# One kernel, three orders: forms of the gate stage, tile products of the output projection, and the forms that open the feed-forward stage

## The chip, the cores and the metric

The kernel runs on one core of a Trainium2 chip. The metric is the device time of one execution in microseconds (us). The time before is the median of three runs, 1219.32 us (1218.68 to 1220.99).

## What is computed

One block of a streaming encoder, in float32, for 1024 tokens and 16 meta tokens ahead of them, 1024 channels wide. Cut to what matters here:

```python
def hybrid_mixer(u, ...):
    z = jnp.einsum('bld,dn->bln', u, w_in)
    a, q, k, v, r, lr, ga, gb = jnp.split(z, IN_SPLITS, axis=-1)
    y_a = ...            # multi-scale pooling of a, mixed, times w_pool_out
    y_b = ...            # chunked gated linear attention of q, k, v, lr; norm; silu(r); times w_gla_out
    m = jax.nn.sigmoid(ga) * y_a + jax.nn.sigmoid(gb) * y_b
    return jnp.einsum('bld,de->ble', m, w_out)

def squared_relu_mlp(u, w_ff1, w_ff2):
    hdn = jnp.square(jax.nn.relu(jnp.einsum('bld,df->blf', u, w_ff1)))
    return jnp.einsum('blf,fd->bld', hdn, w_ff2)

h = h + hybrid_mixer(rmsnorm(h, norm_mix), ...)
h = h + squared_relu_mlp(rmsnorm(h, norm_ffn), w_ff1, w_ff2)
return rmsnorm(h, norm_final)[:, N_META:]
```

`w_ff1` is 1024 x 4096 and `w_ff2` 4096 x 1024. The change touches three stages: the first product with `w_in` (its gate columns), the product of `m` with `w_out`, and the first products with `w_ff1`.

## The kernel before

**Split products.** Every float32 operand is split into a high part that TensorE takes and a low part, the rest. ScalarE (ACT) makes the high part by a copy, VectorE (DVE) the low part by a subtraction: for weights these are `split` (L267 high, L268 low) and, for `w_out`, L1572 and L1573. A product is three matmuls for each of four blocks of the contraction, high by high, high by low and low by high (`mm3`, L249 to L251). A product of a 128-row tile with 512 columns is thus twelve matmuls.

**Seven products for eight.** The large products are done on quarters of the matrices with seven products in place of eight, P1 to P7, from sums and differences of quarters. `Quarters` does this for `w_in`'s gate columns and for `w_ff1`, column block by column block: P3.1 is the third product of block 1. `Quarters.order` lists the products; `sums` makes the sum or difference of weights that each needs on DVE, `forms` splits it, and loads the next weights once a form has freed their place (`load`, on SyncE's queue, SP, L300). The results are joined on DVE: P6 gives `u2p` (L400), P7 gives `u3p` (L405), and P3, P4 and P5 are added to these (`c`, L868, in the gate stage; `acc`, L1915, in the feed-forward stage). A form can only be written once the products of the form four places before it have been read.

**The output projection.** It runs between the attention and the feed-forward stage, token tile by token tile (0 to 3 are one half of the tokens, 4 to 7 the other). `PLAN` is a list of steps in the order in which they are given to all engines; ACT and DVE run in that order, and SP's loads do as well. In it `P1.0` is the first product of tile 0. P1 and P2 share a bank (`b[t]`), so do P5 and P3, and P7 and P4. `T1` to `T4` are sums of quarters of `w_out`, made earlier in memory (`wt_dram`); `ldT4.0` loads a half of one (L1563), always into the same two places (`rawx`, `u2p`), `T4.0a` makes its high part on ACT and `T4.0` its low part on DVE. `S1` to `S4` are sums of the tokens' quarters (L1674), `fS` their split parts (L1657 and L1664). `u` (L1768, ACT) takes a partial sum out of its bank; `C11` (L1678), `l5`, `l3`, `l7` (L1698), `a4` and `U2` (L1694) join products into `acc`; `x` and `ldx` bring in the rows of `x`, `x.4` to `x.7` by an adding DMA on GpSimd's queue (POOL). `s3` splits a tile of `s3` (L1707 low, L1709 high). `sq`, `ln` and `nm` are the norm of a tile (its last step is L241, on DVE), `t0` to `t7` its transposes on TensorE (L1807), the `e` steps the transposed parts and forms (L1809 ACT, L1810 DVE), `x4` the form of P4 (`t4h`, `t4l`, L1752). `F.0` and on are steps of the feed-forward loop: one product each, in `Quarters.order`'s order, so F.8 is P3.0, F.9 P6.1, and F.10 P4.0. `sm`, `pr` and `prl` make its weight forms: sum, high part, low part.

**Queues.** SP issues loads in the program's order. Ahead of the output projection it issued rows 0 and 3 of `x` (`behind_third`, L1855), `gB`, the gain of the norm (`load_gB`, L1551), and then T2; in the queue T4 stood behind the first two loads of `w_ff1` (`first_blocks`).

## Time and profile before

| | |
|---|---|
| median of three runs | 1219.32 us |
| the profiled execution | 1217.28 us |
| its span, first to last instruction | 1215.3 us |
| granted TensorE clock, mean | 0.997 |
| ACT busy | 648.7 us (53%) |
| POOL busy | 75.9 us (6%) |

The profiled execution is 2.0 us longer than its span and 2.0 us shorter than the median. The span is made of stages: the product with `w_in` with the gate columns first, the pooling and the attention, the output projection from about 490 to 590 us, and the feed-forward stage from about 588 us to the end. Times of the trace are counted from the span's start. A row of the timeline has the start, the length, the engine, the line and the operation, and in brackets how long the engine had stood idle and what ended that. An engine that is busy all the time sets the pace; an idle time counts only where that engine is the one.

### The profile page before, as it was taken

What the parts mean: (1) busy time and instruction counts of PE and PEld (TensorE: products, weight loads), DVE (VectorE), ACT (ScalarE), POOL (GpSimd) and SP (SyncE); (2) the same over time, 40 slices, a digit from 0 to 9 for tenths busy, and PEclk for the clock granted to TensorE, in tenths of its full rate; (3) what the DMA queues carried; (4) which work ended last, traced back from release to release, by engine and by line L of the source; (5) the groups of instructions that cost most, each with busy time, mean ns of one, the idle gap of its engine ahead of it and who ended that gap; (6) DMA issues with size and microseconds to landing.
All of it is one profiled execution on the core that took longest, in us unless ns stands there. A gap on an engine that the chain in (4) does not pass through costs nothing.

```text
span 1215.3 us, 18460 instructions
## 1 busy us (share of the span) xinstructions
PE 1183.5 (97%) x6762; PEld 986.2 (81%) x6762; DVE 896.9 (74%) x1436; ACT 648.7 (53%) x1176; POOL 75.9 (6%) x122
## 2 busy tenths in 40 slices
PE   9989999999999999989989999999999999999997
PEld 8878888898988877768768888888888888888886
DVE  7987577666677877777887667676675887887686
ACT  7677567745446433438745455454454444444554
POOL 2200010000102244010000000000000000000000
PEclk9999999999999999999999999999999999999999
DMA  8246783545108577972235444454479963333532
GB/s 256 36 113 171 218 193 120 156 122 164 37 19 279 195 246 231 355 185 112 97 121 171 145 162 156 130 166 145 166 259 322 329 232 96 96 96 95 173 96 87
DMA packets 149514, 199.02 MB, mean 164 GB/s; under 512 B 10712, under 2 KB 81136, under 8 KB 148624
## 3 DMA queue, kind: packets, MB, share of 16 engines
q1 hardware_dynamic: 144144, 181.79, 46.1%
q0 software_dynamic: 5120, 15.80, 5.7%
q8 instruction: 53, 0.87, 0.3%
q14 instruction: 37, 0.30, 0.1%
q10 hardware_dynamic: 160, 0.27, 0.1%
HBM read 138.04 MB, written 68.16 MB: 170 GB/s over the span
## 4 chain that ended last, share of the span: by engine, by line
PE 84%; DVE 6%; DMA 5%; ACT 2%; issue 1%; SPq 0%; POOL 0%; DVEq 0%; ACTq 0%; POOLq 0%
PE b_ms L250 9%; PE b_ms L251 9%; PE b_ms L249 9%; PE b_mm L249 9%; PE b_mm L251 9%; PE b_mm L250 9%; PE b_x L250 7%; PE b_x L249 7%; PE b_x L251 7%; DMA rawx<-wt_dram 2%; DMA o<-ma_dram 1%; PE b_sc L1326 1%; DMA plain_dram<-t 1%; PE b_mx L249 1%; PE b_mx L251 1%
## 5 line engine op out<-in xcount | busy, mean ns | idle before, releaser
L249 PE MATMUL b_mm<-th,w1h 128*128 128x512 f32 (+1 forms) x308 | 115.5, 375 | 5.0 <-DVE c L868 3.1
L251 PE MATMUL b_mm<-th,w1l 128*128 128x512 f32 (+1 forms) x308 | 114.2, 371 | 0.0
L250 PE MATMUL b_mm<-tl,w1h 128*128 128x512 f32 (+1 forms) x308 | 114.1, 371 | 0.0
L249 PE MATMUL b_x<-th,w1h 128*128 128x512 f32 (+1 forms) x264 | 100.2, 380 | 0.0
L250 PE MATMUL b_x<-tl,w1h 128*128 128x512 f32 (+1 forms) x264 | 100.1, 379 | 0.0
L251 PE MATMUL b_x<-th,w1l 128*128 128x512 f32 (+1 forms) x264 | 99.7, 378 | 0.0
L267 ACT ACTIVATE w1h<-raw 128x512 fp32r<-128x512 f32 x98 | 60.8, 620 | 26.8 <-PE b_ms L250 14.3
L267 ACT ACTIVATE w1h<-fs 128x512 fp32r<-128x512 f32 x78 | 49.0, 628 | 46.5 <-PE b_ms L250 27.1
L268 DVE TENSOR_TENSOR w1l<-raw,w1h 128x512 fp32r<-128x512 f32 x98 | 67.1, 685 | 8.3 <-ACT w1h L267 8.3
L249 PEld LDWEIGHTS b_mm<-th,w1h 128*128 128x128 f32 x308 | 57.8, 188 | 16.3 <-issue 6.2
L251 PEld LDWEIGHTS b_mm<-th,w1l 128*128 128x128 f32 x308 | 57.9, 188 | 10.1
L250 PEld LDWEIGHTS b_mm<-tl,w1h 128*128 128x128 f32 x308 | 57.9, 188 | 9.6
L267 ACT ACTIVATE w1h<-bt 128x512 fp32r<-128x512 f32 x44 | 27.8, 632 | 66.8 <-issue 62.5
L268 DVE TENSOR_TENSOR w1l<-fs,w1h 128x512 fp32r<-128x512 f32 x78 | 53.5, 685 | 13.4 <-ACT w1h L267 13.4
L251 PEld LDWEIGHTS b_x<-th,w1l 128*128 128x128 f32 x264 | 49.6, 188 | 9.5
L249 PEld LDWEIGHTS b_x<-th,w1h 128*128 128x128 f32 x264 | 49.6, 188 | 9.5
L250 PEld LDWEIGHTS b_x<-tl,w1h 128*128 128x128 f32 x264 | 49.6, 188 | 9.3
L1978 DVE TENSOR_TENSOR bt<-w,w 128x512 f32<-128x512 f32 x80 | 54.7, 684 | 0.3 <-DMA w<-in_w_ff_dram 0.3
L267 ACT ACTIVATE fxh<-bt 128x512 fp32r<-128x512 f32 x36 | 22.8, 632 | 56.0 <-issue 50.4
L1917 ACT ACTIVATE acc<-acc 128x512 f32<-128x512 f32 x48 | 30.3, 631 | 34.0 <-DVE acc L1915 34.0
L268 DVE TENSOR_TENSOR w1l<-rawx,w1h 128x512 fp32r<-128x512 f32 x44 | 30.1, 687 | 24.4 <-ACT w1h L267 24.4
L267 ACT ACTIVATE w1h<-rawx 128x512 fp32r<-128x512 f32 x44 | 27.5, 626 | 35.0 <-PE b_ms L250 19.9
(535 smaller groups left out, 3424.1 us busy)
## 6 DMA issues: line engine op xcount, KB each, us to landing
hf_dram<-acc SPq DMA_DIRECT2D x112, 256.0 KB, 2.1
raw<-hf_dram SPq DMA_DIRECT2D x112, 256.0 KB, 2.6
w<-in_w_ff_dram SPq DMA_DIRECT2D x64, 256.0 KB, 4.5
raw<-in_w_in_dram SPq DMA_DIRECT2D x22, 512.0 KB, 4.5
raw<-in_w_ff_dram SPq DMA_DIRECT2D x16, 512.0 KB, 4.1
rawx<-in_w_ff_dram SPq DMA_DIRECT2D x16, 512.0 KB, 4.2
wt_dram<-in_w_out_dram POOLq DMA_DIRECT2D x6, 1024.0 KB, 11.0
rawx<-in_w_in_dram SPq DMA_DIRECT2D x10, 512.0 KB, 4.4
```

The costliest lines, as they stand in the source:

```text
L249: pe.matmul(ps, ah, bh, start=first and i == 0, stop=False, skip_group_check=more)
L250: pe.matmul(ps, ah, bl, start=False, stop=False, skip_group_check=more)
L251: pe.matmul(ps, al, bh, start=False, stop=last and i == n - 1, skip_group_check=more)
L267: act.activation(hi, a, ACT.Copy)
L268: low = lambda: dve.tensor_tensor(lo, a, f32(hi), ALU.subtract)
L1326: pe.matmul(b[to, e, j], kk[r, s], qq[r, s], start=True, stop=True, tile_position=(e * CH, u * CH))
L1917: act.activation(h[w], b, ACT.Relu)
L1978: dve.tensor_tensor(bt, w, S["w2"][q[3:]][:, i], ALU.add if q[2] == "+" else ALU.subtract)
```

## The change

Three orders are changed, and some loads with them; no product is added or left out.

- **Gate stage.** `Quarters.order` gives the first products as P6.0, P7.0, P4.0, P3.0, P6.1, P1.2, where it was P6.0, P7.0, P3.0, P6.1, P4.0, P1.2. The load of the next weights' second half then waits for P3.0's form and no longer for P4.0's.
- **Feed-forward stage.** With the new flag `moved`, which is set for this stage alone, the order is P6.0, P7.0, P3.0, P6.1, P7.1, P4.0, P1.2: P7.1 now stands ahead of P4.0, where it followed P1.2. `PLAN` therefore holds one step more, F.11, which is P4.0.
- **Output projection.** `PLAN` is listed anew. The products run P1, P2, P6, P5.0, P5.1, P7.0, P3.0, P3.1, P5.2, P4.0, t0, P7.1, t1, P3.2, t4, P5.3, P4.1, t2, P7.2, P3.3, P7.3, t5, P4.2, t3, P4.3, F.0; before, P5 and P3 of all four tiles stood ahead of P7 and P4. `u.1` and `u.2` stand ahead of T2's parts; `C11.2`, `C11.3` and `C11.0` stand together, behind P2's products, and `C11.1` alone behind T4's first part.
- **Loads.** T2 goes ahead of rows 0 and 3 of `x`; `gB` goes between rows 2 and 1; T4 goes ahead of the first two loads of `w_ff1`.

```diff
@@ Quarters.order @@
-            yield from (("P6", 0), ("P7", 0), ("P3", 0), ("P6", 1), ("P4", 0))
+            moved = (("P6", 0), ("P7", 0), ("P3", 0), ("P6", 1), ("P7", 1), ("P4", 0))
+            yield from moved if self.moved else ((p, 0) for p in ("P6", "P7", "P4", "P3"))
             for i in range(2, self.n + 1):
-                for p in ("P6", "P1", "P7", "P5", "P4", "P2", "P3")[i == 2 :]:
+                for p in ("P6", "P1", "P7", "P5", "P4", "P2", "P3"):
+                    if self.moved and (p, i - 1) in moved:
+                        continue
...
@@ Quarters.forms @@
-                if p == ("P3" if i else "P4") and i + 2 < self.n:
+                if p == ("P4" if self.moved and not i else "P3") and i + 2 < self.n:
                     self.load(i + 2, 1)
...
-    def load_gB():
+    def no_more():
         late()
-        nc.sync.dma_start(gB, bcast(norm_ffn))
...
@@ PLAN @@
-        P5.0 U2.3 xU.3 nU.3 T3.0 x.6 P5.1 T3.1 s3.0a ldT4.0 l5.0 ldT4.1 C11.2 C11.3 P3.0 s3.1a l5.1 x.7 s3.0
...
+        B22.0 P5.0 x.5 ldT4.1 B22.1 U2.2 P5.1 xU.2 s3.0a U2.3 nU.2 s3.0 T4.0a x.6 l5.0 nU.3 T4.0 P7.0 T4.1a
+        C11.1 s3.1a T4.1 P3.0 l7.0 l5.1 s3.1 xU.3 P3.1 l3.0 x.7 sq.0 hd.0 ln.0 P5.2 l3.1 hd.1 sq.1 nm.0 ln.1
...
@@ out_projection @@
         for q in range(2):
             fetch("T2", q, places[q])
+        for t in (0, 3):
+            nc.sync.dma_start(acc[:, t], x[t * P : (t + 1) * P, :])
...
+            elif name == "gain":
+                nc.sync.dma_start(gB, bcast(norm_ffn))
...
+        for n in list(prime_lows):
+            prime_lows.pop(n)()
         any_order("order")
@@ first_blocks @@
+        ff_quarters.moved = True
         ff_quarters.places = [raw.own, [S["rawx0"], None]]
@@ behind_third @@
-        for t in (0, 3):
-            nc.sync.dma_start(S["acc"][:, t], x[t * P : (t + 1) * P, :])
```

**Gate stage, TensorE.** Behind the last matmuls of P7.0 (`P7h`, `P7l` are its token parts) stood P3.0 (`th_146`, `tl_150`):

```order
L249 MATMUL b_ms<-P7h,w1h 128x512
L250 MATMUL b_ms<-P7l,w1h 128x512
L251 MATMUL b_ms<-P7h,w1l 128x512
L249 MATMUL b_mm<-th_146,w1h 128x512
L250 MATMUL b_mm<-tl_150,w1h 128x512
```

Now P4.0 (`P4h`, `P4l`) stands there:

```order
L251 MATMUL b_ms<-P7h,w1l 128x512
L249 MATMUL b_ms<-P4h,w1h 128x512
L250 MATMUL b_ms<-P4l,w1h 128x512
L251 MATMUL b_ms<-P4h,w1l 128x512
L249 MATMUL b_ms<-P4h,w1h 128x512
L250 MATMUL b_ms<-P4l,w1h 128x512
```

All twelve matmuls of P4.0 moved ahead of P3.0 and P6.1.

**Output projection, SP.** The loads before, from `gB` on (`rawx` and `u2p` from `wt_dram` are the halves of T2, T1, T3 and T4 in this order; `raw` is `w_ff1`):

```order
L1551 DMA gB<-in_norm_ffn_dram 128x1024
L1563 DMA rawx_5104<-wt_dram 128x2x512
L1563 DMA u2p<-wt_dram 128x2x512
L1686 DMA acc<-in_x_dram 128x1024 x2
L1563 DMA rawx_5104<-wt_dram 128x2x512
L1563 DMA u2p<-wt_dram 128x2x512
L1563 DMA rawx_5104<-wt_dram 128x2x512
L1563 DMA u2p<-wt_dram 128x2x512
L300 DMA raw_122<-in_w_ff_dram 128x8x128
L300 DMA raw_126<-in_w_ff_dram 128x8x128
L1563 DMA rawx_5104<-wt_dram 128x2x512
```

And now:

```order
L1565 DMA rawx_5101<-wt_dram 128x2x512
L1565 DMA u2p<-wt_dram 128x2x512
L1763 DMA acc<-in_x_dram 128x1024 x2
L1688 DMA acc<-in_x_dram 128x1024
L1789 DMA gB<-in_norm_ffn_dram 128x1024
L1688 DMA acc<-in_x_dram 128x1024
L1565 DMA rawx_5101<-wt_dram 128x2x512
L1565 DMA u2p<-wt_dram 128x2x512
L1565 DMA rawx_5101<-wt_dram 128x2x512
L1565 DMA u2p<-wt_dram 128x2x512
L1565 DMA rawx_5101<-wt_dram 128x2x512
L1565 DMA u2p<-wt_dram 128x2x512
```

T2 moved ahead of the rows of `x` and of `gB`, and T4 (the last two loads here) ahead of `w_ff1`.

**Output projection, DVE.** Around the joins of P1 and P2 (L1678) before (L1573 are T3's and T4's low parts, `ww` and `wz`; L1698 `l5` and `l3`; L1707 `s3`):

```order
L1698 TENSOR_TENSOR acc<-acc,b_mm 128x512
L1678 TENSOR_TENSOR acc<-b_x,acc 128x512
L1678 TENSOR_TENSOR acc<-b_mm,acc 128x512
L1698 TENSOR_TENSOR acc<-acc,b_mm 128x512
L1707 TENSOR_TENSOR tl_150<-sums,th_146 128x4x128 x2
L1573 TENSOR_TENSOR wz<-rawx_5104,wz 128x1024
L1698 TENSOR_TENSOR acc<-acc,b_mm 128x512
L1573 TENSOR_TENSOR wz<-u2p,wz 128x1024
L1698 TENSOR_TENSOR acc<-acc,b_mm 128x512
L241 SCALAR_TENSOR_TENSOR u_5108<-acc,small,gB 128x1024
```

And now, where the lines are three or two higher (L1680 is the join, L1575 T4's low part, L1700 `l5` and `l7`, L1709 `s3`):

```order
L1696 TENSOR_TENSOR acc<-u_5105,b_ms 128x512
L1709 TENSOR_TENSOR tl_150<-sums,th_146 128x4x128
L1700 TENSOR_TENSOR acc<-acc,b_mm 128x512
L1575 TENSOR_TENSOR wz<-rawx_5101,wz 128x1024
L1680 TENSOR_TENSOR acc<-b_x,acc 128x512
L1575 TENSOR_TENSOR wz<-u2p,wz 128x1024
L1700 TENSOR_TENSOR acc<-acc,b_x 128x512
L1700 TENSOR_TENSOR acc<-acc,b_mm 128x512
L1709 TENSOR_TENSOR tl_150<-sums,th_146 128x4x128
L1684 TENSOR_TENSOR acc<-acc 128x512
```

The joins of three tiles moved ahead (they are not in this piece); the first part of `s3` stands ahead of `l5.0`, and behind T4's first part stand one join, T4's second part, `l7.0` and `l5.1`.

**Start of the feed-forward stage, DVE.** From P6.0's result (`u2p`) to P3.0's (the first `acc<-b_mm,u3p`) before:

```order
L400 TENSOR_TENSOR u2p<-b_ms,u2p 128x512
L336 TENSOR_TENSOR fs<-fs,rawx_5104 128x512
L268 TENSOR_TENSOR w1l<-fs,w1h 128x512
L1810 TENSOR_TENSOR acc<-acc 128x512 x2
L405 TENSOR_TENSOR u3p<-b_ms,u2p 128x512
L1915 TENSOR_TENSOR acc<-b_mm,u3p 128x512
L1922 TENSOR_TENSOR acc<-acc 128x512
```

And now:

```order
L403 TENSOR_TENSOR u2p<-b_ms,u2p 128x512
L268 TENSOR_TENSOR w1l<-fs,w1h 128x512
L339 TENSOR_TENSOR fs<-fs,rawx_5101 128x512
L342 TENSOR_TENSOR s_5762<-rawx_5101,rawx_5778 128x512
L1818 TENSOR_TENSOR acc<-acc 128x512
L268 TENSOR_TENSOR w1l<-fs,w1h 128x512
L408 TENSOR_TENSOR u3p<-b_ms,u2p 128x512
L344 TENSOR_TENSOR fs<-rawx_5101,fs 128x512
L1922 TENSOR_TENSOR acc<-b_mm,u3p 128x512
L1929 TENSOR_TENSOR acc<-acc 128x512
```

Between the two results stand a low part (L268), a weight sum (L342) and a weight difference (L344) that were not there, and one step on `acc` (L1818) fewer.

## The prediction

> **What bounds the kernel now.** I read the page's busy shares and the chain's shares first, then the list of what TensorE (PE) waits for, then windows around its waits, and at last the timelines there.

> ```profile
> PE 1183.5 (97%) x6762; PEld 986.2 (81%) x6762; DVE 896.9 (74%) x1436; ACT 648.7 (53%) x1176; POOL 75.9 (6%) x122
> PE 84%; DVE 6%; DMA 5%; ACT 2%; issue 1%; SPq 0%; POOL 0%; DVEq 0%; ACTq 0%; POOLq 0%
> ```

> PE is busy for 97% of the span and holds 84% of the chain that ended last. The change adds and removes no matmul, so only PE's remaining idle time, and time at a lowered clock, can be gained. The list of PE's waits says where that is (line, tile, what ended the wait; us in total, times, longest):

> ```profile
> PE b_mm L249 <- DVE acc L1678: 4.9, 1, 4.9
> PE b_mm L249 <- DVE c L868: 3.1, 1, 3.1
> PE b_ms L250 <- DVE t4l L1752: 2.8, 1, 2.8
> PE b_x L249 <- ACT u L1768: 2.2, 1, 2.2
> PE b_mm L249 <- DVE acc L1915: 2.0, 1, 2.0
> PE b_ms L1807 <- DVE u L241: 1.4, 1, 1.4
> PE b_mm L249 <- DVE acc L1698: 1.0, 1, 1.0
> PE b_ms L251 <- DVE w1l L268: 0.9, 1, 0.9
> ```

> All eight lie at the three places that the change reorders, and they make 18.3 us. The windows (from:to and length; busy time of PE, PEld, DVE, ACT, POOL; granted clock; DMA share, GB/s) show the rest:

> ```profile
> 500.00:540.00 40.00, 32.10 (x136) 25.79 (x136) 38.08 (x41) 18.23 (x22) 3.48 (x4) 0.98 0.73 226
> 539.00:541.00 2.00, 2.00 (x6) 1.52 (x6) 0.00 (x0) 0.00 (x0) 0.00 (x0) 0.50 1.07 215
> 590.00:633.00 43.00, 35.84 (x161) 28.29 (x160) 36.36 (x59) 26.66 (x51) 0.00 (x0) 1.00 0.30 96
> 600.00:610.00 10.00, 10.00 (x45) 8.26 (x44) 10.00 (x18) 6.89 (x12) 0.00 (x0) 1.00 0.14 54
> 640.00:1200.00 560.00, 560.00 (x2472) 463.46 (x2471) 411.25 (x665) 270.57 (x470) 0.00 (x0) 1.00 0.51 165
> ```

> From 640 us on PE never stops, so what is won before that reaches the end. In the two earlier windows DVE is nearly as full as PE: it is the engine that can take over the bound.

> **The change, part by part.** One product is twelve matmuls at the pitch of these rows, 0.227 us: 2.72 us.

> Gate stage:

> ```profile
> 69.07 0.39 PE L251 MATMUL b_ms<-P7h,w1l 128*128 128x512 f32 x1
> 72.51 0.47 PE L249 MATMUL b_mm<-th,w1h 128*128 128x512 f32 x1 [3.06 <-DVE c L868]
> 78.07 0.39 PE L249 MATMUL b_ms<-P4h,w1h 128*128 128x512 f32 x1
> 80.79 0.40 PE L249 MATMUL b_x<-th,w1h 128*128 128x512 f32 x1
> 65.20 2.36 DVE L823 TENSOR_TENSOR P4l<-ut,P4h 128x1024 fp32r<-128x1024 f32 x2
> 71.68 0.68 DVE L868 TENSOR_TENSOR c<-b_mm,u3p 128x512 f32<-128x512 f32 x1
> ```

> P3.0 waits for `c`, which frees its bank. P4.0's token parts are made by 67.5, and its weights' low part takes the next place but one on DVE, ready at about 68.7. So P4.0 runs from 69.3 to 72.0 in the gap. On DVE as many 0.60 us steps stand between `P4l` and `c` as before, so `c` still comes at 71.7 and P3.0 starts at 72.5. P1.2 then starts one product earlier, at 78.07 in place of 80.79: **2.7 us**. The load now tied to P3.0's form goes out about 7 us later, and P1.2 starts 2.7 us earlier, so 10 us of its slack go; the page's part on DMA issues gives its landing:

> ```profile
> rawx<-in_w_in_dram SPq DMA_DIRECT2D x10, 512.0 KB, 4.4
> ```

> Issued at some 68.4 it is there by 73, ahead of 78.07, and I cost it at nothing; with that cover gone it returns up to 2.7. Bounds: 0 to 3.1, the whole wait.

> Output projection, up to F.0:

> ```profile
> 510.94 0.58 ACT L1768 ACTIVATE u<-b_x 128x512 f32<-128x512 f32 x1
> 533.25 0.39 PE L251 MATMUL b_mm<-wx,tl 128*128 128x512 f32 x1
> 538.56 0.80 PE L249 MATMUL b_mm<-wx,th 128*128 128x512 f32 x1 [4.92 <-DVE acc L1678]
> 542.89 0.39 PE L249 MATMUL b_mm<-w1h,th 128*128 128x512 f32 x1
> 523.32 0.68 DVE L1678 TENSOR_TENSOR acc<-b_mm,acc 128x512 f32<-128x512 f32 x1
> 535.49 1.22 DVE L1573 TENSOR_TENSOR ww<-u2p,ww 128x1024 fp32r<-128x1024 f32 x1
> 537.82 0.68 DVE L1678 TENSOR_TENSOR acc<-b_mm,acc 128x512 f32<-128x512 f32 x1
> 543.14 0.69 DVE L1698 TENSOR_TENSOR acc<-acc,b_mm 128x512 f32<-128x512 f32 x1 [4.64 <-issue]
> 509.97 1.06 ACT L1572 ACTIVATE wz<-rawx 128x1024 fp32r<-128x1024 f32 x1 [2.71 <-DMA rawx<-wt_dram]
> 516.63 1.06 ACT L1572 ACTIVATE wx<-rawx 128x1024 fp32r<-128x1024 f32 x1 [0.35 <-DMA rawx<-wt_dram]
> 513.01 0.38 SPq L1563 DMA_DIRECT2D rawx<-wt_dram x1
> 535.60 0.74 SPq L1563 DMA_DIRECT2D rawx<-wt_dram x1
> 546.51 1.06 ACT L1572 ACTIVATE wz<-rawx 128x1024 fp32r<-128x1024 f32 x1 [3.02 <-DMA rawx<-wt_dram]
> ```

> *Gone.* `u.1` stood on ACT behind T2's first part, which stood behind a load; it now stands ahead of it, and T2 is asked for first: 2.2. P5.1 waited for `C11.3`, listed late at 537.82; all joins but one now stand in DVE's list right behind T1's parts, so 4.9 go. P5.1 also ran slowly behind that wait, from 538.56 to 542.89, 4.33 for 2.72, at a clock of 0.50: another 1.6. The 1.0 of L1698 belongs to the old order and goes. Together 9.7.

> *New, P7.0.* P5.1 now ends at 534.0: P5.0 ended at 533.48, 2.72 on, less the 2.2 gained ahead. P7.0 stands next and its third matmul, at 534.4, needs the low part of `s3.0`. On DVE, from the joins at 523.32, this comes behind 10 steps of 0.60 (a 128x512 step's pitch: three joins, four `U2`, three `xU`) and 6 of 1.14 (a 128x1024 step's, as the joins at 537.82 and the last `ww` at 535.49 stand 2.33 apart with two 0.60 steps between: two parts of `fS4`, four of T3 and B22), which is 12.8, and takes 0.60: 536.8. PE waits 2.4. Bounds: 0, if DVE starts the list earlier, to 4.9, the wait that it replaces. Behind P7.0 in PE's queue stand P3.0, P3.1, P5.2, all wanted at once.

> *New, P3.1.* P7.0 ends at 539.2, P3.0 at 541.9. P3.1 waits for `l5.1`, on DVE behind T4's first part, `C11.1`, T4's second part and `l7.0`. T4 is free to load when T3's parts are read, about 531, 4.5 earlier than at 535.60. In flight it was 3.6 in quiet (513.01 to 516.63, T1) and 10.9 behind the two `w_ff1` loads (535.60 to 546.51); these are now behind it, `x.4` to `x.7` still beside it. I take 6.3, nearer the quiet row: landing at 537.3, high part 538.4, then 1.14, 0.60, 1.14 (its half lands about 1.1 later), 0.60 and 0.60: 542.6, and 0.2 to PE. PE waits 1.0. Bounds 0 to 5.6, by the two times in flight. Behind it in the queue stand P5.2 and P4.0.

> From there to t5, followed step by step at these pitches, each operand is ready some half a microsecond ahead or more; I cost these steps at nothing, and a cover gone costs what the old L1698 wait cost, about 1.0 a place. The rows of `x` and `gB` now stand behind T2; their readers are the joins from 523.32 on and the norms behind, while T1, which follows them on SP, went out at 513.01: nothing. So F.0 comes 9.7 - 3.4 = **6.3 us** earlier.

> Start of the feed-forward stage:

> ```profile
> 615.06 0.47 PE L249 MATMUL b_mm<-th,w1h 128*128 128x512 f32 x1 [1.95 <-DVE acc L1915]
> 625.11 0.50 PE L250 MATMUL b_ms<-t4l,w1h 128*128 128x512 f32 x1 [2.83 <-DVE t4l L1752]
> 616.28 0.69 DVE L1922 TENSOR_TENSOR acc<-acc 128x512 f32<-128x512 f32 x1 [1.36 <-ACT acc L1918]
> 621.35 0.69 DVE L1929 TENSOR_TENSOR acc<-acc 128x512 f32<-128x512 f32 x1 [0.77 <-ACT acc L1918]
> ```

> Here DVE bounds. DVE's list starts 6.3 earlier, but two more 0.60 steps stand between `u2p` and the result that P3.0 waits for: it is 5.1 earlier, 610.0. PE arrives 6.3 and some 0.5 (less of t7's 1.4) before 613.1, at 606.3: F.8's wait grows from 1.95 to about 3.7. From there to `t4l` DVE has one step less but no step to put behind the second 0.77 of ACT's answer, so `t4l` stays 5.1 earlier, 620.0. PE meanwhile runs P3.0, P6.1 without the 0.9 of `w1l`, and now P7.1, to 618.2; P4.0 waits 1.6 in place of 2.8. It resumes 5.1 earlier with P7.1's 2.7 done: 7.8. I leave 0.9 for P5.2's low weights behind `t4l` (the row of L268; bounds 0 to 1.8). So the two stages together give **6.9 us**, the order of P7.1 itself 0.6 of it; alone it is bounded by -2 (DVE's two steps and the clock) and +2.7.

> *Sum:* 2.7 + 6.9 = 9.6. The profiled execution took 1217.28 (its span of 1215.3 and 2.0 around it), so 1207.7 by its own time; the median shown is 2.04 above it, which gives 1209.7, **1210** with the digit that these sums bear.

> **The rivals.**

> *T4 lands late again.* The DMA share in 539 to 541 is 1.07: the engines were full. With 10.9 in flight T4 lands at 541.9, P3.1 waits 5.6 and not 1.0, and the total gain is 5.0: 1214.3; if the clock falls as it did behind 4.9, 1215.9. For it: POOL's four adding loads stay beside T4. Against: the 1 MB of `w_ff1` now comes behind. [...]

> *F.8's wait lowers the clock.* The wait of 4.92 was followed by 1.6 lost at 0.50; behind 3.06 P3.0 and P6.1 took 5.56 (72.51 to 78.07), where two products at full pitch take 5.44. F.8's forecast 3.7 lies between: with the loss, 1211.3. [...]

> *Nothing arrives.* DVE's busy 38.08 of 40 leaves it 1.9 idle in that window (part of the 4.64 behind 538.5), and 36.36 of 43 leaves 6.6 in the later one. If new orders stall DVE for as much as PE's waits lose, DVE bounds throughout and only the gate's 2.7 or less stays: 1217 to 1219.5. Against: the 4.64 is DVE waiting for PE, which is what the early joins cure.

> *Slower.* DVE stands in order behind T4's first part with everything that PE needs next. Each microsecond of landing beyond 537.3 costs one at P3.1, and 1.6 for the clock. The 9.6 are spent when T4 lands at 545.3, 14.3 in flight; at 20 in flight the time is 1225. Before, the longest was 10.9, with 1 MB ahead; so this is unlikely.

> **How the numbers follow.** Forecast (1207.5 to 1212.5, the clock rival in it at 0.2): 0.67. T4 late: 0.18 (1213 to 1216). Nothing arrives: 0.08. Slower: 0.04. Better still, with P7.0's and P3.1's waits at their lower bounds, down to 1205: 0.03. The range leaves out the last three: 1206 to 1216. A measurement of this kernel tells about 0.2% from no change, 2.4 us, so faster is below 1216.9: 0.90; within it 0.06; slower 0.04.

> **What would show it.** Right: no wait on `c` in the gate stage with P4.0 in its place; no wait of P5.1 and no clock of 0.50 near 535; a wait of 1.5 to 3.5 at P7.0's third matmul for a low part of `s3`, about 1 at P3.1; some 3.7 at F.8 for `acc`, 1.6 at P4.0 for `t4l`. Wrong: P1.2 waiting for a load in the gate stage; T4 in flight for 10; DVE idle behind T4 for over 4; waits on `l` joins or on `t` steps from 545 to 580 that I costed at nothing; PE idle beyond 640.

## The result, and the profile after

The changed kernel takes 1208.41 us (median of 4 runs, 1207.65 to 1209.88); the kernel before, beside it, 1219.0 us. The ratio is 0.9912, with a 95% interval from 0.9895 to 0.9929: 10.7 us faster. Forecast were 1210, and 1206 to 1216. The profiled execution took 1207.65 us, 9.6 less than the profiled one of before. One execution of a later experiment, T4_behind_wff1, took 3060.32 us where its eight others took 1212 to 1216, and is left out of its ratio.

From the page after the change, the busy shares and the chain's shares by engine:

```profile
PE 1183.8 (98%) x6762; PEld 988.5 (82%) x6762; DVE 895.9 (74%) x1436; ACT 647.1 (54%) x1176; POOL 75.7 (6%) x122
PE 83%; DVE 6%; DMA 4%; ACT 3%; issue 2%; POOL 1%; SPq 0%; POOLq 0%; DVEq 0%; ACTq 0%
```

PE's work is the same; it is done in 9.6 us less. From the list of PE's waits after the change, those at the reordered places and the one that is new, to be held against the list in the prediction (us in total, times, longest):

```profile
PE b_mm L249 <- DVE acc L1922: 4.4, 2, 4.1
PE b_mm L249 <- ACT w1h L84: 1.4, 1, 1.4
PE b_x L251 <- DVE tl L1709: 1.3, 1, 1.3
PE b_ms L1815 <- ACT acc L1817: 1.0, 1, 1.0
PE b_mm L249 <- DVE acc L1700: 1.0, 1, 1.0
PE b_mm L251 <- DVE w1l L268: 0.6, 1, 0.6
PE b_mm L249 <- DVE c L871: 0.3, 1, 0.3
PE b_ms L250 <- DVE t4l L1754: 0.2, 1, 0.2
```

The waits on the joins (4.9), on `c` (3.1), on `t4l` (2.8) and on `u` (2.2) are gone or nearly so. One has grown, that of F.8 on `acc` (2.0 to 4.1), and one is new that no part of the change touches: `w1h`, L84.

The windows after (columns as in the prediction):

```profile
541.00:584.00 43.00, 43.00 (x219) 36.10 (x217) 34.76 (x50) 35.40 (x95) 0.86 (x1) 1.00 0.40 133
595.00:605.00 10.00, 7.67 (x34) 6.01 (x32) 9.87 (x17) 3.73 (x7) 0.00 (x0) 1.00 0.26 81
608.00:611.00 3.00, 3.00 (x9) 2.32 (x8) 3.00 (x5) 1.64 (x3) 0.00 (x0) 0.50 0.92 315
640.00:1190.00 550.00, 549.72 (x2426) 455.03 (x2425) 403.40 (x653) 264.57 (x461) 0.00 (x0) 1.00 0.51 164
```

PE is full through the rest of the projection; around 600 us DVE is (9.87 of 10) and PE waits; from 608 to 611 the clock is 0.50; behind 640 PE is full again, so that a lead there reaches the end.

Where the time went is read by taking one matmul in both timelines and subtracting its starts; the difference is called the lead. First the rows of after in the gate stage (P4.0 in P3.0's gap, P3.0, P1.2), then those at a `y_b` product ahead of the projection:

```profile
69.66 0.39 PE L249 MATMUL b_ms<-P4h,w1h 128*128 128x512 f32 x1
72.84 0.47 PE L249 MATMUL b_mm<-th,w1h 128*128 128x512 f32 x1 [0.30 <-DVE c L871]
78.38 0.40 PE L249 MATMUL b_x<-th,w1h 128*128 128x512 f32 x1
...
479.91 0.50 PE L249 MATMUL b_mm<-yg,w1h 128*128 128x512 f32 x1 [1.40 <-ACT w1h L84]
481.17 0.67 PE L251 MATMUL b_mm<-yg,w1l 128*128 128x512 f32 x1 [0.53 <-DVE w1l L88]
484.63 0.45 PE L250 MATMUL b_mm<-yg,w1h 128*128 128x512 f32 x1
```

Of the same three places, before had P1.2 at 80.79 and these two rows for the matmuls of 479.91 and 484.63:

```profile
482.67 0.50 PE L249 MATMUL b_mm<-yg,w1h 128*128 128x512 f32 x1
485.88 0.39 PE L250 MATMUL b_mm<-yg,w1h 128*128 128x512 f32 x1
```

The gate stage wins 2.4 (80.79 - 78.38). Small waits between 453 and 473 raise this to 4.1, but the weights of the `y_b` product come only 2.8 earlier (482.67 - 479.91), and behind the two waits the matmuls run slowly (the clock is 0.50 from 481.3 to 484.7): at 484.63 the lead is 1.25.

The other places after: P7.0's third matmul, P3.1, F.0, F.8 and two later matmuls of it (the last is the end of the slow ones), P4.0, P5.2; and T4's first load with its high part:

```profile
533.30 0.50 PE L251 MATMUL b_x<-ww,tl 128*128 128x512 f32 x1 [1.27 <-DVE tl L1709]
539.54 0.50 PE L249 MATMUL b_mm<-w1h,th 128*128 128x512 f32 x1 [0.95 <-DVE acc L1700]
577.78 0.39 PE L249 MATMUL b_x<-th,w1h 128*128 128x512 f32 x1
606.78 0.47 PE L249 MATMUL b_mm<-th,w1h 128*128 128x512 f32 x1 [4.11 <-DVE acc L1922]
608.34 0.63 PE L251 MATMUL b_mm<-th,w1l 128*128 128x512 f32 x1
610.90 0.47 PE L251 MATMUL b_mm<-th,w1l 128*128 128x512 f32 x1
617.22 0.50 PE L250 MATMUL b_ms<-t4l,w1h 128*128 128x512 f32 x1 [0.17 <-DVE t4l L1754]
623.83 0.50 PE L251 MATMUL b_mm<-th,w1l 128*128 128x512 f32 x1 [0.62 <-DVE w1l L268]
527.35 0.36 SPq L1565 DMA_DIRECT2D rawx<-wt_dram  x1
534.24 1.06 ACT L1574 ACTIVATE wz<-rawx 128x1024 fp32r<-128x1024 f32 x1 [2.19 <-DMA rawx<-wt_dram]
```

F.0 began at 587.71 before:

```profile
587.71 0.39 PE L249 MATMUL b_x<-th,w1h 128*128 128x512 f32 x1
```

So the lead grows from 1.25 to 9.9 through the projection, is 8.3 at F.8 (615.06 - 606.78), and 10.6 at P4.0 (625.11 - 617.22, and P7.1's 2.7 is done there). P5.2's wait and a little later take it to 9.6 at the end.

### The profile page after: what moved, and what is told of

It reads as the page before. It is cut to its first block, busy times and chain, and to the rows that moved or that the text cites. A ratio compares the mean times of both kernels' runs of the same rounds, so it can differ in the third digit from the quotient of the medians.

```text
span 1205.7 us, 18471 instructions
## 1 busy us (share of the span) xinstructions
PE 1183.8 (98%) x6762; PEld 988.5 (82%) x6762; DVE 895.9 (74%) x1436; ACT 647.1 (54%) x1176; POOL 75.7 (6%) x122
## 4 chain that ended last, share of the span: by engine, by line
PE 83%; DVE 6%; DMA 4%; ACT 3%; issue 2%; POOL 1%; SPq 0%; POOLq 0%; DVEq 0%; ACTq 0%
PE b_mm L249 10%; PE b_mm L251 9%; PE b_mm L250 9%; PE b_ms L250 9%; PE b_ms L251 9%; PE b_ms L249 9%; PE b_x L250 7%; PE b_x L249 7%; PE b_x L251 7%; PE b_sc L1329 1%; PE b_mx L249 1%; PE b_mx L251 1%; PE b_mx L250 1%; DMA t<-gb_dram 1%; DMA raw<-in_w_out_dram 1%
## 5 line engine op out<-in xcount | busy, mean ns | idle before, releaser
L249 PE MATMUL b_mm<-th,w1h 128*128 128x512 f32 (+1 forms) x308 | 116.2, 377 | 4.7 <-DVE acc L1922 4.4
L251 PE MATMUL b_mm<-th,w1l 128*128 128x512 f32 (+1 forms) x308 | 114.9, 373 | 0.6 <-DVE w1l L268 0.6
L250 PE MATMUL b_mm<-tl,w1h 128*128 128x512 f32 (+1 forms) x308 | 114.8, 373 | 0.0
L250 PE MATMUL b_x<-tl,w1h 128*128 128x512 f32 (+1 forms) x264 | 100.1, 379 | 0.0
L249 PE MATMUL b_x<-th,w1h 128*128 128x512 f32 (+1 forms) x264 | 100.1, 379 | 0.0
L251 PE MATMUL b_x<-th,w1l 128*128 128x512 f32 (+1 forms) x264 | 99.7, 378 | 0.0
L268 DVE TENSOR_TENSOR w1l<-raw,w1h 128x512 fp32r<-128x512 f32 x98 | 67.0, 684 | 8.6 <-ACT w1h L267 8.6
L249 PEld LDWEIGHTS b_mm<-th,w1h 128*128 128x128 f32 x308 | 58.1, 189 | 16.0 <-issue 5.9
L251 PEld LDWEIGHTS b_mm<-th,w1l 128*128 128x128 f32 x308 | 58.3, 189 | 11.3 <-DVE w1l L268 1.0
L250 PEld LDWEIGHTS b_mm<-tl,w1h 128*128 128x128 f32 x308 | 58.2, 189 | 9.7
L268 DVE TENSOR_TENSOR w1l<-fs,w1h 128x512 fp32r<-128x512 f32 x78 | 53.4, 685 | 14.9 <-ACT w1h L267 14.8
L251 PEld LDWEIGHTS b_x<-th,w1l 128*128 128x128 f32 x264 | 49.6, 188 | 9.5
L249 PEld LDWEIGHTS b_x<-th,w1h 128*128 128x128 f32 x264 | 49.6, 188 | 9.5
L250 PEld LDWEIGHTS b_x<-tl,w1h 128*128 128x128 f32 x264 | 49.6, 188 | 9.3
L268 DVE TENSOR_TENSOR w1l<-rawx,w1h 128x512 fp32r<-128x512 f32 x44 | 30.1, 686 | 25.3 <-ACT w1h L267 25.3
## 6 DMA issues: line engine op xcount, KB each, us to landing
raw<-in_w_in_dram SPq DMA_DIRECT2D x22, 512.0 KB, 4.7
raw<-in_w_ff_dram SPq DMA_DIRECT2D x16, 512.0 KB, 4.2
rawx<-in_w_ff_dram SPq DMA_DIRECT2D x16, 512.0 KB, 4.1
rawx<-in_w_in_dram SPq DMA_DIRECT2D x10, 512.0 KB, 4.4
```

The costliest lines, as they stand in the source:

```text
L249: pe.matmul(ps, ah, bh, start=first and i == 0, stop=False, skip_group_check=more)
L250: pe.matmul(ps, ah, bl, start=False, stop=False, skip_group_check=more)
L251: pe.matmul(ps, al, bh, start=False, stop=last and i == n - 1, skip_group_check=more)
L268: low = lambda: dve.tensor_tensor(lo, a, f32(hi), ALU.subtract)
```

## The experiments

The part of each of the three orders comes first, then the loads and joins of the projection, then DVE's list and the clock at F.8 and in the gate stage, and at last a version that may be better. Ratios are to the kernel before; 0.001 is 1.2 us.

**gate_alone.** The kernel before with the gate stage's new order alone.

```diff
-            yield from (("P6", 0), ("P7", 0), ("P3", 0), ("P6", 1), ("P4", 0))
+            first = (("P6", 0), ("P7", 0), ("P3", 0), ("P6", 1), ("P4", 0))
+            yield from first if self.moved else ((p, 0) for p in ("P6", "P7", "P4", "P3"))
...
-                if p == ("P3" if i else "P4") and i + 2 < self.n:
+                if p == ("P4" if self.moved and not i else "P3") and i + 2 < self.n:
...
```

> The kernel before with the gate stage's new order alone (P4.0 ahead of P3.0); output projection and feed-forward as before. Theory, from the two traces: P1.2 starts 2.4 us earlier, but the y_b products before the output projection depend on a chain that gains less, so PE waits there for w1h (L84) and the lead shrinks to 1 to 2 us: 1217 to 1218. Rival A: the lead of 2.4 to 2.7 goes through: 1216.4. Rival B: the DMA chain ahead of the output projection (o from ma_dram, then T2) does not move at all: 1219.

Measured: 1214.88, ratio 0.9963 (0.9949 to 0.9977): 4.5 us, by the interval 2.8 to 6.2. The theory's 1 to 2 is out, and rival A's 2.4 to 2.7 lies just below the interval; the gain is about the whole wait of 3.1 on `c`, or more. Why it can be more is seen in the next kernels.

**ff_alone.** The kernel before with P7.1 ahead of P4.0 in the feed-forward stage.

```diff
-            yield from (("P6", 0), ("P7", 0), ("P3", 0), ("P6", 1), ("P4", 0))
+            first = (("P6", 0), ("P7", 0), ("P3", 0), ("P6", 1), ("P4", 0))
+            first = first[:4] + (("P7", 1),) + first[4:] if self.moved else first
+            yield from first
...
```

> The kernel before with P7.1 ahead of P4.0 in the feed-forward stage alone. Theory: P7.1 fills the wait of 2.8 for t4l; P7.1's weight sum now stands on DVE ahead of P3.0's bank, so F.8's wait grows by 0.6 and t4l comes up to 0.6 later: 1.5 to 2.1 gained, 1217 to 1217.5. Rival: DVE's added steps delay t4l by as much as P7.1 fills: 1219.

Measured: 1217.01, ratio 0.9977 (0.9966 to 0.9988): 2.8 us, by the interval 1.5 to 4.1, which takes in the theory's 1.5 to 2.1 and not the rival. Its gate stage is that of before. In its timeline there, P3.0's first matmul, a later one, and one of P6.1:

```profile
72.57 0.47 PE L249 MATMUL b_mm<-th,w1h 128*128 128x512 f32 x1 [3.04 <-DVE c L872]
...
74.07 0.63 PE L249 MATMUL b_mm<-th,w1h 128*128 128x512 f32 x1
...
77.44 0.39 PE L251 MATMUL b_ms<-P6h,w1l 128*128 128x512 f32 x1
```

The wait is as long as before, but here it is followed by slow matmuls (0.63 long) from 74 to 77.4, which cost 1.6; before's profiled execution had none there. The wait of 3 us therefore costs 3 in some runs and 4.6 in others: of the five profiled executions that keep it at its full length, the slow matmuls follow in two (this one and no_gate's) and not in three (those of before, proj_alone and joins_early_alone).

**no_gate.** The changed kernel with the gate stage's old order.

```diff
-            moved = (("P6", 0), ("P7", 0), ("P3", 0), ("P6", 1), ("P7", 1), ("P4", 0))
-            yield from moved if self.moved else ((p, 0) for p in ("P6", "P7", "P4", "P3"))
+            first = (("P6", 0), ("P7", 0), ("P3", 0), ("P6", 1), ("P4", 0))
+            first = first[:4] + (("P7", 1),) + first[4:] if self.moved else first
+            yield from first
...
```

> The changed kernel with the gate stage's old order; the rest as changed. Theory: the gate's order is worth only what is left of its lead at the output projection, 1 to 2 us: 1209.4 to 1210.4. Rival A: it is worth 2.4 to 2.7: 1211. Rival B: nothing: 1208.4.

Measured: 1212.06, ratio 0.9935 (0.9919 to 0.9951). Against the changed kernel's 0.9912 that is 2.8 us for the gate's order (0.0023), rival A's size; the two intervals overlap, so this kernel alone doesn't exclude the theory. The window of one us at 74 in this kernel's gate stage has the clock at 0.50 as well:

```profile
74.00:75.00 1.00, 1.00 (x3) 0.78 (x3) 0.27 (x1) 0.97 (x2) 0.00 (x0) 0.50 0.83 248
```

**proj_alone.** The changed kernel with both orders of products of before: the projection's list and loads alone.

```diff
-            moved = (("P6", 0), ("P7", 0), ("P3", 0), ("P6", 1), ("P7", 1), ("P4", 0))
-            yield from moved if self.moved else ((p, 0) for p in ("P6", "P7", "P4", "P3"))
+            yield from (("P6", 0), ("P7", 0), ("P3", 0), ("P6", 1), ("P4", 0))
...
-                if p == ("P4" if self.moved and not i else "P3") and i + 2 < self.n:
+                if p == ("P3" if i else "P4") and i + 2 < self.n:
```

> The changed kernel with both orders of products of before (gate stage and feed-forward stage); the new list of the output projection and its loads stay. Theory: the projection gains 8 to 9 us up to F.0, and the start of the feed-forward stage, where DVE bounds and P4.0 has no product to cover its wait for t4l, gives back about 2: 1212 to 1213. Rival: nothing is given back, the feed-forward order adds nothing: 1210.

Measured: 1215.92, ratio 0.997 (0.9959 to 0.9982): 3.7 us, by the interval 2.2 to 5.0, less than the theory's 6 to 7. Its timeline at F.8 and P4.0:

```profile
609.40 0.77 PE L249 MATMUL b_mm<-th,w1h 128*128 128x512 f32 x1 [3.75 <-DVE acc L1919]
621.23 0.69 PE L250 MATMUL b_ms<-t4l,w1h 128*128 128x512 f32 x1 [3.32 <-DVE t4l L1751]
```

Both waits grew (from 1.95 and 2.83), and both first matmuls are slow. P4.0 has no product ahead of it there to cover its wait; with P7.1 in that place (the kernel before this one) it waits 0.2. The three parts alone make 4.5 + 2.8 + 3.7 = 11.0 beside 10.7 for all.

**joins_early_alone.** The kernel before with C11.2 and C11.3 behind C11.0 and C11.1.

```diff
-        T1.1a fS1.0 fS1.1 P2.3 T1.0 T1.1 ldT3.0 P6.0 fS4.0a C11.0 fS4.1a ldT3.1 C11.1 fS4.0 B22.0a P6.1
+        T1.1a fS1.0 fS1.1 P2.3 T1.0 T1.1 ldT3.0 P6.0 fS4.0a C11.0 fS4.1a ldT3.1 C11.1 C11.2 C11.3 fS4.0 B22.0a P6.1
...
-        P5.0 U2.3 xU.3 nU.3 T3.0 x.6 P5.1 T3.1 s3.0a ldT4.0 l5.0 ldT4.1 C11.2 C11.3 P3.0 s3.1a l5.1 x.7 s3.0
+        P5.0 U2.3 xU.3 nU.3 T3.0 x.6 P5.1 T3.1 s3.0a ldT4.0 l5.0 ldT4.1 P3.0 s3.1a l5.1 x.7 s3.0
```

> The kernel before with the joins C11.2 and C11.3 listed right behind C11.0 and C11.1, nothing else. Theory: P5.1's wait of 4.9 goes, but DVE then stands behind T4's first part, which still lands at some 546 to 548, with l3.0 behind it, so PE runs P3.0 and P3.1 early and waits for P5.2's bank instead: 0 gained, up to 2 lost to the two steps and to the clock: 1219 to 1221. Rival, the prediction's reading: the early joins cure the wait by themselves, 4.9 plus 1.6 less some 1: 1213 to 1214.

Measured: 1220.8, ratio 1.0017 (1.0005 to 1.0029): nothing gained, a little lost. Its timeline at P3.0 and P5.2, and DVE's first step on T4:

```profile
537.95 0.47 PE L249 MATMUL b_mm<-w1h,th 128*128 128x512 f32 x1 [0.68 <-DVE acc L1698]
549.66 0.79 PE L249 MATMUL b_mm<-wx,th 128*128 128x512 f32 x1 [6.00 <-DVE acc L1698]
547.79 1.23 DVE L1573 TENSOR_TENSOR wz<-rawx,wz 128x1024 fp32r<-128x1024 f32 x1 [8.18 <-ACT wz L1572]
```

P5.1's wait of 4.9 has gone and P5.2 waits 6.0 instead, until 549.66, where it began at 549.48 before: DVE stood idle for 8.18 behind T4's first part, and the join that P5.2 needs (`l3.0`) comes behind that part. The rival, the prediction's reading, is out.

**T4_behind_wff1.** The changed kernel with T4's loads behind the first two of `w_ff1`.

```diff
-        P6.1 fS4.0 B22.1a U2.0 T3.0a xU.0 fS4.1 P6.2 nU.0 x.4 T3.1a U2.1 xU.1 nU.1 T3.0 P6.3 T3.1 ldT4.0
-        B22.0 P5.0 x.5 ldT4.1 B22.1 U2.2 P5.1 xU.2 s3.0a U2.3 nU.2 s3.0 T4.0a x.6 l5.0 nU.3 T4.0 P7.0 T4.1a
+        P6.1 fS4.0 B22.1a U2.0 T3.0a xU.0 fS4.1 P6.2 nU.0 x.4 T3.1a U2.1 xU.1 nU.1 T3.0 P6.3 T3.1
+        B22.0 P5.0 x.5 B22.1 ffl U2.2 P5.1 xU.2 s3.0a U2.3 nU.2 s3.0 ldT4.0 ldT4.1 T4.0a x.6 l5.0 nU.3 T4.0 P7.0 T4.1a
...
+            elif name == "ffl":
+                first_loads()
...
```

> The changed kernel with T4's loads back behind the first two loads of w_ff1 in SP's queue. Theory: T4's first part is 10 to 11 us in flight in place of 6.9, so DVE and then P3.1 wait some 4 us longer and a window of lowered clock (1.6) comes with it; part of the 5.6 comes back at F.8, whose wait of 4.1 shrinks, since DVE is the bound there. Net 2 to 4 lost: 1210.5 to 1212.5. Rival: the w_ff1 loads are not what kept T4 in flight, POOL's loads are: T4 in 7, time 1208.4.

Measured: 1213.81, ratio 0.995 (0.9936 to 0.9963): 4.6 us of the 10.7 are lost, more than expected. SP's two issues, T4's two high parts on ACT, and P5.2 on PE:

```profile
531.53 1.39 SPq L1565 DMA_DIRECT2D rawx<-wt_dram  x1
533.03 0.41 SPq L1565 DMA_DIRECT2D u2p<-wt_dram  x1
538.72 1.06 ACT L1574 ACTIVATE wz<-rawx 128x1024 fp32r<-128x1024 f32 x1 [6.47 <-DMA rawx<-wt_dram]
542.42 1.06 ACT L1574 ACTIVATE wz<-u2p 128x1024 fp32r<-128x1024 f32 x1 [2.12 <-DMA u2p<-wt_dram]
546.60 0.50 PE L249 MATMUL b_mm<-wx,th 128*128 128x512 f32 x1 [3.49 <-DVE acc L1700]
```

The first part is in flight for 7.2, hardly longer than the 6.9 of after and near the rival's 7, not the theory's 10 to 11; but it is issued 4.2 later (527.35 before this edit). The second lands 6.7 later (535.72 in after): it is issued 4.6 later (528.48 in after) and flies 9.4 in place of 7.2. P5.2 pays. F.8's wait stays 4.12, so nothing comes back there, against the theory.

**loads_as_before.** The changed kernel with T2 behind rows 0 and 3 of `x` and `gB`; `u.1` stays ahead of T2's parts.

```diff
         late()
+        nc.sync.dma_start(gB, bcast(norm_ffn))
...
-        for t in (0, 3):
-            nc.sync.dma_start(acc[:, t], x[t * P : (t + 1) * P, :])
         rota["mm"] = ("mm",)
...
+        for t in (0, 3):
+            nc.sync.dma_start(S["acc"][:, t], x[t * P : (t + 1) * P, :])
```

> The changed kernel with T2 behind rows 0 and 3 of x and gB, as before; u.1 stays ahead of T2's parts in the list. Theory: P2.1 has no wait either way, that is u.1's place; but T2's low parts stand in DVE's full list, so a T2 that lands 2 to 3 us later delays the list, and P7.0 waits longer for s3 (up to 4 in place of 1.3 to 2.8): 1 to 3 lost, 1209.5 to 1211.5. Rival: the early T2 brings nothing: 1208.4.

Measured: 1207.37, ratio 0.9901 (0.9881 to 0.9921), not to be told from the changed kernel. P2.1 does not wait in it; P7.0's third matmul waits 2.75, within the 1.3 to 2.8 of the other traces. The rival holds: `u.1`'s place removed the 2.2, the early load of T2 brings nothing that can be measured.

**short_list_F8.** The changed kernel with fewer DVE steps ahead of P3.0's bank and `t4`'s low parts ahead of P3.0's results.

```diff
-        F.7 prl.8 sm.9 sm.10 pr.9a e5.x4 pr.10a prl.9 F.8 x4.1a prl.10 sm.11 pr.11a e6.x4 e7.x4 x4.2a prl.11
-        F.9 x4.3a x4.0 sm.12 pr.12a x4.1 x4.2 x4.3 F.10 prl.12 sm.13 pr.13a F.11
+        F.7 prl.8 sm.9 pr.9a F.8 prl.9 sm.10 e5.x4 pr.10a x4.1a prl.10 sm.11 pr.11a e6.x4 e7.x4 x4.2a prl.11
+        x4.3a x4.0 x4.1 x4.2 x4.3 F.9 sm.12 pr.12a F.10 prl.12 sm.13 pr.13a F.11
```

> The changed kernel with a shorter DVE list at two places of the feed-forward start: of the four steps ahead of P3.0's bank three stand behind it, and the low parts of t4 stand ahead of P3.0's own results. Theory: DVE bounds there, so F.8 waits 2 in place of 4.1, P4.0 less than 0.5, and t4l is ready about 4 us earlier; with at most one window of lowered clock fewer the gain is 2.5 to 5: 1203.5 to 1206. Rival: the wait moves to P5.2's low weights and its bank, and nothing is gained: 1208.4.

Measured: 1209.94, ratio 0.9922 (0.9905 to 0.9938): nothing gained. PE's rows at F.8 and behind it:

```profile
604.57 0.47 PE L249 MATMUL b_mm<-th,w1h 128*128 128x512 f32 x1 [1.84 <-DVE acc L1922]
618.64 0.50 PE L251 MATMUL b_x<-th,w1l 128*128 128x512 f32 x1 [1.62 <-DVE w1l L268]
624.87 0.50 PE L251 MATMUL b_mm<-th,w1l 128*128 128x512 f32 x1 [3.20 <-DVE w1l L268]
```

F.8's wait fell by 2.3 as meant, and low parts (`w1l`) are then late by 1.6 and 3.2, as the rival said: the steps put off are wanted a little later. This order wins nothing here. That DVE's sum of work bounds the stretch, whatever its order, is likely and not shown: it is one order, and from 600 to 630 DVE is busy for 26.0 of 30 in after and for 25.3 here.

**filler_at_F8.** The changed kernel with one product more than needed, into a bank that nobody reads, in F.8's wait.

```diff
                 yield
+                if self.moved and (p, i) == ("P7", 0):
+                    mm3(bank("ms"), 4, lambda k: (ah[:, k], al[:, k]), lambda k: (bh[:, k], bl[:, k]))
```

> The changed kernel with one product more than needed, twelve matmuls into a bank that nobody reads, between P7.0 and P3.0 of the feed-forward start, where PE waits 4.1. Theory: the clock falls for one 3.4 us window behind any such window in which PE was idle for over some 2 us, and this costs 1.6 by itself; with the filler PE is idle for 1.4 only, P3.0 runs at full pitch and the time falls by 1 to 1.7: 1206.7 to 1207.4. Rival: the added product costs nothing and brings nothing, since the wait sets the time and not the clock: 1208.4.

Measured: 1208.85, ratio 0.9907 (0.9891 to 0.9924), as the changed kernel. F.8 and P4.0 on PE:

```profile
606.39 0.47 PE L249 MATMUL b_mm<-th,w1h 128*128 128x512 f32 x1 [1.40 <-DVE acc L1924]
616.43 0.50 PE L250 MATMUL b_ms<-t4l,w1h 128*128 128x512 f32 x1 [1.36 <-DVE t4l L1756]
```

The added matmuls fill the wait, 1.40 in place of 4.11, and no slow matmuls follow in this trace: here it is the idle time, not the change of stage, that the slow matmuls go with. But P4.0 now waits 1.36 in place of 0.17: what the clock costs at F.8, DVE hides.

**filler_at_gate.** The same with the kernel before, in the gate stage's wait on `c`.

```diff
                 yield
+                if (p, i) == ("P7", 0) and self.n != NPAIR:
+                    mm3(bank("ms"), 4, lambda k: (ah[:, k], al[:, k]), lambda k: (bh[:, k], bl[:, k]))
```

> The kernel before with one product more than needed, twelve matmuls into a bank that nobody reads, in the gate stage between P7.0 and P3.0, where PE waits 3.1 for c. Theory: a 3.4 us window with over some 2 us of idle PE is followed by one at half clock, which costs 1.6; a wait of 3.1 makes such a window in about three runs of four, so the added product costs nothing and saves 1.2 on average: 1217.8 where before is 1219.0, and in its trace no matmul of P3.0 or P6.1 is slow. Rival: it saves nothing, the clock is not set by this idle time: 1219.0.

Measured: 1218.32 beside 1219.43, ratio 0.9993 (0.9979 to 1.0006). The sign is the theory's, but the interval holds both; P3.0 and P6.1 ran at full pitch in its trace, as they did in one of before. In time this is undecided.

**s3_l5_early** and **changed_again.** `s3.0` ahead of B22's second part and `l5.1` ahead of T4's; beside it, on the same chip, the changed kernel itself.

```diff
-        B22.0 P5.0 x.5 ldT4.1 B22.1 U2.2 P5.1 xU.2 s3.0a U2.3 nU.2 s3.0 T4.0a x.6 l5.0 nU.3 T4.0 P7.0 T4.1a
-        C11.1 s3.1a T4.1 P3.0 l7.0 l5.1 s3.1 xU.3 P3.1 ...
+        B22.0 P5.0 x.5 s3.0a ldT4.1 s3.0 B22.1 U2.2 P5.1 xU.2 U2.3 nU.2 l5.0 l5.1 T4.0a x.6 nU.3 T4.0 P7.0 T4.1a
+        C11.1 s3.1a T4.1 P3.0 l7.0 s3.1 xU.3 P3.1 ...
```

> The changed kernel with s3.0 listed ahead of B22's second part and U2.2, and l5.1 ahead of T4's parts. Theory: P7.0's wait for s3 (1.3 to 2.8) and P3.1's for l5.1 (1.0) go, and with them a window of lowered clock in some runs; 1 to 3 gained where DVE does not take it back at F.8: 1205.5 to 1207.5. Rival: T4's landing and DVE's list bound P5.2 and F.8 in any case, and the waits move there: 1208.4.

> The changed kernel itself, on the same chip as the others of this call. Both theories: 0.991 of before.

Measured: 1206.3, ratio 0.9899 (0.988 to 0.9918), and 1208.83, 0.9913 (0.9893 to 0.9933). P7.0 does not wait any more; P3.0 waits 1.06 and P5.2 1.39, both for `l` joins. The medians are 2.5 apart as the theory has it, but the intervals overlap, so it is likely and not shown that this version is the faster.

## Why the prediction was right

Its sum was near (9.6 forecast, 9.6 between the two profiled executions), with terms that erred both ways: up to the projection 1.2 came in place of 2.7, in the projection 8.7 in place of 6.3, behind it -0.3 in place of 0.6. The places and most of the waits were right; that the errors cancel to the digit is luck.

- **Gate, 2.7.** The mechanism is right; between the traces it is 2.4. By time it is worth 4.5 alone and 2.8 in the changed kernel, with wide intervals (2.8 to 6.2 for the first); that a wait of 3 us is also followed by slow matmuls in some runs (two of five traces, 1.6 in ff_alone) can explain the more, but filler_at_gate did not settle it by time. The step costed this wait at its own length, with a rule read from one execution in which nothing followed it. That a part is lost again at `w1h` before the projection was not foreseen, but it belongs to that execution and not to the new order: the wait at this product is 1.47 in ff_alone and 1.27 in no_gate, which have the old order, and is absent in gate_alone and loads_as_before, which have the new one.
- **Gone in the projection, 9.7.** 10.5 went: the four terms, and the 0.8 of P1.2 besides (which loads_as_before, with the same list, still has at 0.73). The reason given for the largest, early joins, is not sufficient: alone they bring nothing. T4 landing early is a condition for it: put late again, it loses 4.6. The prediction took T4's landing to matter for P3.1 and for a rival only; a large part of the projection's gain hangs on it. What the new order of the products adds was not tried apart from T4's earlier load. Of "T2 is asked for first" nothing could be measured.
- **New at P7.0 and P3.1, 3.4.** 1.27 and 0.95 in this trace, 2.2. In the five traces with the changed list that have no slow matmuls between 481 and 489, PE waits 2.7 to 2.8 at P7.0 for DVE's step; in the three that have them (after, changed_again, no_gate) it comes later and waits 1.3 to 2.2. So the 1.27 is one execution's, and the 2.4 forecast is near the usual wait. T4 was in flight for 6.9, where 6.3 were taken.
- **F.0, 6.3 earlier.** 8.7 (1.25 to 9.93). The two points above make 8.3 of it; the rest is not itemized here.
- **Feed-forward start, 0.6.** About -0.3. F.8 waits 4.1 (forecast 3.7), P4.0 0.2 (1.6), P5.2 0.6 (0.9). The clock rival came true at F.8; it cost little, since it took the place of P4.0's wait: the rival added it up as if PE set the pace there, and it is DVE.
- **The median.** 2.04 was carried over from before's profiled execution, which had slow matmuls behind one wait; the traces of gate_alone, ff_alone and joins_early_alone, each with one change from it, have them behind three. For the changed kernel the difference is 0.8.

The rivals: T4 late was priced at 1214.3; its experiment gave 1213.8, but mostly by a later issue, and at P5.2 rather than P3.1, so the price was right by luck. The clock rival came in the trace and not in the time. "Nothing arrives" and "slower" did not come.

## What to carry to other kernels

A wait removed is a gain only if the next thing on the same list is ready too: find what the engine that released it stands behind (here DVE behind a load), and move that first. Where another engine is nearly full through a stretch, a new order within it can merely move the waits (short_list_F8); a product that has to be done anyway, put into the gap, did shorten them (ff_alone). And in these runs a wait of PE of some 2 us and more (1.96 in gate_alone, 3.04 in ff_alone, 4.11 in after) cost its length and, in some of them, 1.6 more in a slow stretch behind it.

## What the runs showed of the hardware

In these runs slow matmuls come in stretches of about 3.4 us (481.3 to 484.7 and 607.6 to 611.0 in after; at times two in a row, as from 549.7 to 555.4 in joins_early_alone) at a clock of 0.50 that cost 1.6 each, and within a run the stretches end on one grid. In gate_alone's timeline, a first and last slow matmul behind F.8's wait of 1.96 and behind P4.0's of 2.67:

```profile
614.36 0.63 PE L249 MATMUL b_mm<-th,w1h 128*128 128x512 f32 x1
617.34 0.44 PE L250 MATMUL b_ms<-forms,w1h 128*128 128x512 f32 x1
...
624.62 0.63 PE L250 MATMUL b_ms<-t4l,w1h 128*128 128x512 f32 x1
627.60 0.44 PE L251 MATMUL b_x<-th,w1l 128*128 128x512 f32 x1
```
